# Ragged self-attention on one core: the four-tile sequences get 64-row projections, a rotation of four PSUM banks and attention in groups of 256 query rows

## The chip, the cores and the metric

The kernel runs on one core of a Trainium2 chip. The metric is the device time of one execution in microseconds (us). It is compared with runs of the kernel before on the same chip; before the change the median is 339.91 us (three runs, 339.87 to 341.66).

## What is computed

There are 32 sequences of random length from 64 to 511, each padded to 512 rows of 512 numbers. For each one the kernel computes Q, K and V, softmax attention in 8 heads of 64, and writes the result; rows beyond the length are zero.

```python
for b in range(batch):
    seq_len = lengths[b]
    x_b = x[b, :seq_len].copy()
    qkv = np.matmul(x_b, w_qkv)                       # 512 -> 3 * 512
    q, k, v = np.split(qkv, 3, axis=-1)               # each to [head, seq, 64]
    scores = scale * np.matmul(q, k.transpose(0, 2, 1))
    attn = np.exp(scores - max) ; attn = attn / (sum + 1e-08)
    output[b, :seq_len] = np.matmul(attn, v) ...      # the rest stays zero
```

The lengths of this case, sorted, are 502 447 446 436 | 363 357 351 347 343 333 323 315 310 261 260 257 | 246 230 223 220 216 183 164 152 143 140 134 119 | 101 86 79 75. The bars part them by how many tiles of 128 rows they fill when taken in pairs: four, three, two and one.

## The kernel before

**Order of work.** The kernel sorts the sequences by length on the chip and handles them in pairs, longest first. A pair runs in a class N, the smallest multiple of 32 (or 340) that holds its longer member; T is N in tiles of 128. Here the classes are 512, 448 (T = 4), 384, 352, 352, 340, 320, 288 (T = 3), 256, 224, 224, 192, 160, 160 (T = 2), 128, 96 (T = 1). The code holds one body per class, and each engine branches from body to body by a register that it loads from the table `cls` (`next_class`, called through `read_class`). A body is two **halves**, one per sequence. In a half the core does the attention of the present sequence (buffers with index h) and, between its steps, the projections of the next one (index g = 1 - h).

**Engines.** TensorE does all matmuls. ScalarE does the exponentials (L344, or L376 in the "dense" T = 3 classes of 340 and less), some casts of Q and K (L407) and half of the output stores. VectorE does the other casts (L408), copies V out of PSUM with the row mask (L431, L479, L499), and normalises the attention output (reciprocal L574, products L593 and L595). GpSimd casts the next x to fp16; SyncE issues the loads, transposes x by DMA into `xT`, and issues the other stores.

**PSUM.** There are eight banks: four in two score slots, `psc` (s0 and s1, two banks each), two in `pa` (a0, a1), two in `pav` (v0, v1). Each has a semaphore that says it was read out: `acquire` makes TensorE wait for it (shown as `e_a0` and so on), `evacuate` raises it.

**The order in a half** is a string of tokens, `ORDER[T]`, or `DENSE`. All engines follow it, each in its own queue:

- `S` is one score unit: for head pair i and key tile kt, two 64-row matmuls over N columns that run side by side (two heads), then one exponential over both banks. Units run i = 1, 2, 3 of this sequence and then i = 0 of the next one. They alternate between s0 and s1, so a unit waits for the exponential of the unit two before it. `D` is a whole dense head pair.
- `Qi` and `Ki` project head pair i of Q or K: four 128-row matmuls over N columns. A small letter has the cast done by ScalarE, a capital one by VectorE.
- `Vi` projects V for key tile i: four 128-row matmuls over 512 columns.
- `Ai` is attention times V for head pair i: per tile of 128 query rows and head, one 65-column matmul per key tile (V has a column of ones for the sum). `+Ai` spreads these between the matmuls of the token before it.
- `O` is the first output store on ScalarE's queue.
- `Ei`/`Fi` .. `Ii` (and `Ui`/`Wi` for V) project two groups at once in 64-row matmuls into two banks: `cross_begin` does rows 0 to 63 of the contraction for one bank side by side with rows 64 to 127 for the other, `cross_end` waits for the semaphore `s_cross` and does the other halves. Only T = 3 used them.

For T = 4 the string before (32 matmuls of the projections of Q and K are 128-row, banks a0 and a1 take turns, attention of a head pair fills both banks of `pav`):

```python
4: "S S Q0 +A0 S S K0 V0 S S Q1 +A1 S S K1 V1 S S Q2 +A2 S S K2 V2 S S Q3 +A3 S S V3 K3 O",
3: "k3 S S E0 E2~ S F0 S I2 S A0 A1 S U0 S S W0 E1~ S S G1 A2 Q3 O A3 S S V2",
DENSE = "K2 q2 D E1 E3 I1 H3 D k0 A0 Q0~ A1 D V2 O V1 A2 D A3~ V0"
```

T = 3 takes its banks "in turns": `pick` pops the bank that has been free longest from the list a0, a1, v0, v1, `give` puts it at the end.

For T = 1 the order is written out in `half`: Q and K of the next sequence in a0 and a1 (which swap from half to half), attention, then all of V in the bank that Q had, then the four score units at once.

Before the first body a prologue projects the first sequence; its last token, V3, is read out of a1 by VectorE.

Of the kernel before, what the change touches and what calls it, by code (L numbers as in the profile page):

```python
# [11 lines left out]
ALU = mybir.AluOpType  # L12

P = 128
NH = 8
HD = 64
NPAIR = 4
# [3 lines left out]
STAGE = 256  # L21
FIRST = {4: 20, 3: 20, 2: 20, 1: None}
AGAIN = 2
SECOND = {4: 20, 3: AGAIN, 2: 0, 1: None}
AT_DENSE = 20
# [123 lines left out]
def kernel(  # L149
# [11 lines left out]
    NC = D // P  # L161
# [8 lines left out]
    def sem(name):  # L170
# [92 lines left out]
        for b in banks  # L263
        for g in (("act",) if b[0] == "s" else ("act", "dve"))
    }
# [25 lines left out]
    def group(pr, b, eng, mms, evac):  # L291
        acquire(pr, b)
        close(pr, b, eng, mms, b[0] != "s")
        evacuate(pr, b, eng, evac)
# [172 lines left out]

    def vproj(pr, bank, h, i, T, whole=False):
        b = f"a{bank}"
        mms = []  # L470
        if whole:
            for c in range(NC):
                mms.append(
                    mm(pa[:, bank, :], xT[h][:, c, 0:P], w_r[:, c, 2 * D : 3 * D],
                       c == 0, c == NC - 1)
                )
            group(
                pr, b, "dve", mms,
                lambda e: e.tensor_scalar(  # L479
                    out=v_aug[h][:, 0, :, 0:HD],  # L480
                    in0=pa[:, bank].rearrange("p (h d) -> p h d", d=HD),
                    scalar1=now[0][:, 0, 0:1], scalar2=None, op0=ALU.mult,
                ),
            )
            return
# [11 lines left out]
        group(  # L497
            pr, b, "dve", mms,
            lambda e: e.tensor_tensor(  # L499
                out=v_aug[h][:, 0:T, 2 * i : 2 * i + 2, 0:HD],  # L500
                in0=pa[:, bank, 0 : T * P].rearrange("p (t a d) -> p t a d", a=2, d=HD),
                in1=now[0][:, 0, 0:T].unsqueeze(2).unsqueeze(3).broadcast_to([P, T, 2, HD]),
                op=ALU.mult,
            ),
        )
# [4 lines left out]

    def attnv(pr, h, i, T, late=False, b=None):

# [6 lines left out]
        if b is not None:  # L519
            jobs = [(2 * 74 * qt, i, qt) for qt in range(T)]  # L520
        elif T == 1:
            jobs = [(74 * 2 * j, j, 0) for j in range(NPAIR)]
        elif T == 4:
            jobs = [(256 * qt, i, qt) for qt in range(T)]
        else:
            jobs = [(74 * (4 * qt + 2 * (i % 2)), i, qt) for qt in range(T)]
        mms = []
        for o0, j, qt in jobs:
            for par in range(2):
                o = o0 + par * (HD + 1 if T == 4 else 74)  # L530
# [15 lines left out]
        if b is not None:  # L546
            res = into[:, 0 : 2 * 74 * T].rearrange("p (t a d) -> p t a d", a=2, d=74)
            dst = on[:, i // 2, 0:T, P * (i % 2) : P * (i % 2 + 1)]
            dst = dst.rearrange("p t (a d) -> p t a d", d=HD)
            sh, fin = [T, 2], i % 2 == 1  # L550
        elif T == 4:
# [5 lines left out]
        else:  # L557
# [4 lines left out]
            else:  # L562
                dst = on[:, i // 2, 0:T, :].rearrange("p t (a d) -> p t a d", d=HD)
        rv = rcp[:, i, 0 : sh[0] * sh[1]].rearrange("p (j a) -> p j a", a=sh[1])
        num, den = res[..., 0:HD], res[..., HD]
# [4 lines left out]
        def recip():  # L570
            for j in (0, 1) if T == 1 else (i // 2,) if not each or i % 2 == 0 else ():
                pr.take("dve", s_od[h][j], 16)
            pr.take("dve", full[(name, "dve")])
            pr.add("dve", lambda e: e.reciprocal(out=rv, in_=den).then_inc(s_r, 1))  # L574

        def mult():
            pr.take("dve", s_r)

            if T == 1:
                cuts = [(slice(0, 2), 0)]  # L580
            elif h == 0:
# [37 lines left out]
    def spread_last(pr):  # L619
# [15 lines left out]
    ORDER = {  # L635
# [3 lines left out]
    }  # L639
    DENSE = "K2 q2 D E1 E3 I1 H3 D k0 A0 Q0~ A1 D V2 O V1 A2 D A3~ V0"  # L640

# [4 lines left out]
    def half(pr, h, T, N, W, st, last=False):  # L646
# [11 lines left out]
        if T == 1:  # L658
            start_proj()
            qk(pr, f"a{st['bank']}", g, [(i, 0) for i in range(NPAIR)], W, P)  # L660
            qk(pr, f"a{st['bank'] ^ 1}", g, [(i, 1) for i in range(NPAIR)], W, P, "act")
            pr.take("pe", s_on[h])
            attnv(pr, h, 0, 1)
            vproj(pr, st["bank"], g, 0, 1, True)
            read_class(pr, h)
            acquire(pr, f"a{st['bank'] ^ 1}")
            pr.signals.append(s_xtf[g])
            if last:
                act_store(pr, h, 0, T)
            scores(pr, h, g, 0, 0, 1, W)  # L670
            if not last:
                act_store(pr, h, 0, T)
            st["bank"] ^= 1
            return
# [19 lines left out]
        for tok in toks:  # L694
# [4 lines left out]
            if k in "SD" and turns:  # L699
# [4 lines left out]
                assert units[0][0] in (1, 2) or len(st["seen"]) == len(area)  # L704
            if k == "S":
                i, kt = units.pop(0)
                scores(pr, st["slot"], *((g, i, kt, T, W) if i == 0 else (h, i, kt, T, N)))
                st["slot"] ^= 1
            elif k == "D":
                i = units[0][0]  # L710
                del units[:T]
                scores_dense(pr, *((g, i, W) if i == 0 else (h, i, N)))
            elif k == "A":
                if first:
# [8 lines left out]
                norm[i] = attnv(pr, h, i, T, f"X{i}" in toks, b)  # L723
                if turns:
# [7 lines left out]
            else:  # L732
# [71 lines left out]
    def in_turns(N):  # L804
        return -(-N // P) == 3 and (not is_dense(N) or "E" in DENSE)

# [964 lines left out]
```

## Time and profile before

| what | value |
|---|---|
| median of the runs shown | 339.91 us |
| the profiled execution: its own time / its span | 339.98 us / 338.2 us |
| TensorE clock granted, mean | 0.996 |
| the T = 4 bodies (first score unit to first T = 3 matmul) | 24.57 to 99.33 us |
| the T = 3 bodies, to the first score unit of T = 2 | 99.33 to 240.35 us |
| the T = 1 bodies | from 319.40 us |

1.8 us of the profiled execution lie outside its span. In the rows, times are microseconds from the start of the span. A timeline row reads: start, busy time of the group from its first start to its last end, engine, line, operation, output<-inputs, shapes, count, and in brackets the idle time ahead with what ended it. Matmuls overlap: the next one starts when the columns of the one before have been streamed in, some 0.16 us before that one's row ends. So the pace of TensorE is read from start to start. `64*128` says that a matmul uses 64 rows of the array.

### The profile page before, as it was taken

The page shows a single profiled execution, that of the slowest core. Times are in us where ns is not written, and L with a number is a line of the kernel's source. Part 1 is how long each engine was busy: PE and PEld are TensorE (multiplying, and loading weights), DVE is VectorE, ACT ScalarE, POOL GpSimd, SP SyncE. Part 2 cuts the span into 40 slices and gives each one's busy share as a digit, 9 for nine tenths or more (in the row PEclk, how much of TensorE's full clock was granted, in tenths as well). Part 3 has the DMA queues.
Part 4 walks back from the last instruction along what each step waited for, and adds up shares of the span by engine and source line. Part 5 has one row for each costly group of instructions (what it writes and reads, how often), then busy time and mean ns, then how long its engine had stood idle before and what let it go on. Part 6 is the DMA issues. An engine that isn't in the chain of part 4 may idle for free. (4 is left out here: it accounts for less than half of the span.)

```text
span 338.2 us, 12070 instructions
## 1 busy us (share of the span) xinstructions
PE 326.1 (96%) x4286; PEld 206.7 (61%) x4287; DVE 211.4 (63%) x560; ACT 239.9 (71%) x337; POOL 63.5 (19%) x102
## 2 busy tenths in 40 slices
PE   7999999999999999999999999999999999999992
PEld 2665454555545656566666676667677777776761
DVE  3676567665665566567557556745766666766772
ACT  4568787777779877977877887777776666556541
POOL 3634020202010220220221022012111221121241
PEclk9999999999999999999999999999999999999998
DMA  6977799866855986886787888898898666988731
GB/s 207 349 161 230 205 392 222 287 165 212 162 188 150 286 292 148 268 302 205 221 292 267 191 251 298 154 255 194 213 171 188 203 162 153 185 193 148 180 111 68
DMA packets 82272, 72.10 MB, mean 213 GB/s; under 512 B 40652, under 2 KB 63180, under 8 KB 82196
## 3 DMA queue, kind: packets, MB, share of 16 engines
q1 hardware_dynamic: 70340, 59.61, 67.3%
q10 hardware_dynamic: 11856, 11.54, 9.9%
q8 instruction: 40, 0.66, 0.8%
q14 instruction: 36, 0.29, 0.3%
HBM read 25.32 MB, written 36.70 MB: 183 GB/s over the span
## 5 line engine op out<-in xcount | busy, mean ns | idle before, releaser
L344 ACT ACTIVATE ep<-psc 128x704 f16<-128x704 f32 (+7 forms) x193 | 156.8, 858 | 58.0 <-PE psc L302 41.0
L302 PE MATMUL pa<-xT,w_r 128*128 128x224 f16 (+21 forms) x984 | 134.2, 276 | 2.3 <-PEq L57 0.9
L302 PEld LDWEIGHTS pa<-xT,w_r 128*128 128x128 f16 (+1 forms) x984 | 75.0, 97 | 35.6 <-issue 14.8
L408 DVE CAST qkT<-pa 128x448 f16<-128x448 f32 (+9 forms) x85 | 48.8, 575 | 47.1 <-PE pa L302 46.5
L302 PE MATMUL pa<-w_r,xT 128*128 128x512 f16 (+3 forms) x348 | 69.9, 346 | 0.0
L302 PE MATMUL psc<-qkT 64*128 64x352 f16 (+17 forms) x702 | 66.9, 287 | 1.2 <-ACT ep L376 0.5
L302 PE MATMUL pav<-v_aug,ep 128*128 128x65 f16 x1414 | 62.1, 194 | 0.0
L302 PEld LDWEIGHTS pav<-v_aug,ep 128*128 128x128 f16 x1414 | 55.4, 98 | 9.3 <-issue 1.1
L1610 POOL CAST v_aug<-masks 128x24 f16 (+4 forms) x33 | 9.1, 276 | 244.5 <-POOLq L1239 244.5
L595 DVE SCALAR_TENSOR_TENSOR onat<-pav,masks,rcp 128x128 f32<-128x128 f32 (+2 forms) x137 | 48.2, 391 | 5.2 <-DVE rcp L574 2.1
L376 ACT ACTIVATE ep<-psc 128x960 f16<-128x960 f32 (+3 forms) x48 | 43.4, 962 | 10.7 <-PE psc L302 7.5
L431 DVE TENSOR_TENSOR v_aug<-pa,masks 128x512 f16<-128x512 f32 (+1 forms) x58 | 39.0, 677 | 17.9 <-PE pa L302 16.9
L1605 POOL CAST x<-x_nat 128x1536 f16<-128x1536 f32 (+3 forms) x33 | 42.1, 1274 | 9.8 <-POOLq L1239 9.3
L302 PEld LDWEIGHTS psc<-qkT 64*128 64x128 f16 x702 | 25.6, 94 | 29.7 <-issue 20.8
L302 PE MATMUL pav<-xT,w_r 64*128 64x352 f16 (+10 forms) x328 | 43.6, 300 | 0.0
L302 PEld LDWEIGHTS pa<-w_r,xT 128*128 128x128 f16 (+1 forms) x348 | 26.0, 97 | 22.3 <-issue 4.4
L407 ACT CAST qkT<-pa 128x352 f16<-128x352 f32 (+7 forms) x58 | 26.5, 462 | 16.0 <-ACTq L57 8.5
L302 PEld LDWEIGHTS pav<-xT,w_r 64*128 64x128 f16 (+1 forms) x328 | 23.6, 95 | 9.4 <-issue 1.1
L574 DVE RECIPROCAL rcp<-pav 128x8 f32<-128x8 f32 (+1 forms) x71 | 14.1, 198 | 22.6 <-PE pav L302 17.2
L302 PE MATMUL pav<-w_r,xT 128*128 128x512 f16 (+2 forms) x84 | 20.7, 374 | 0.0
L302 PEld LDWEIGHTS pa<-v_aug,ep 128*128 128x128 f16 x378 | 13.6, 98 | 4.2 <-issue 1.8
L593 DVE TENSOR_TENSOR onat<-pav,rcp 128x256 f32<-128x256 f32 (+1 forms) x32 | 14.6, 458 | 1.1
(77 smaller groups left out, 132.8 us busy)
## 6 DMA issues: line engine op xcount, KB each, us to landing
out_dram<-zt SPq DMA_DIRECT2D x16, 768.0 KB, 5.8
x_nat<-in_x_dram SPq DMA_DIRECT2D x12, 512.0 KB
x_nat<-in_x_dram SPq DMA_DIRECT2D x5, 1024.0 KB
out_dram<-onat ACTq DMA_DIRECT2D x12, 384.0 KB, 5.0
out_dram<-onat SPq DMA_DIRECT2D x12, 384.0 KB, 4.3
x_nat<-in_x_dram SPq DMA_DIRECT2D x17, 256.0 KB, 6.2
out_dram<-onat ACTq DMA_DIRECT2D x16, 256.0 KB, 3.2
x_nat<-in_x_dram SPq DMA_DIRECT2D x4, 768.0 KB
```

The source lines that it names most:

```text
L302: return lambda e: e.matmul(o, lhsT, rhs, start=start, stop=stop)
L344: lambda e: e.activation(out=dst, in_=src, func=AF.Exp, scale=scale),
L376: lambda e, par=par, b=b: e.activation(out=ep[:, i, par, 0:3, 0:N], in_=psc_f[:, par, 0 : 3 * N].rearrange("p (t n) -> p t n", n=N), func= ...
L407: return lambda e: e.copy(out=dst, in_=src)
L408: return lambda e: e.tensor_copy(out=dst, in_=src)
L431: return lambda e: e.tensor_tensor(out=v_aug[h][:, t, lo // HD : lo // HD + n, 0:HD], in0=area[b][:, 0:w].rearrange("p (a d) -> p a d", d=HD),
L574: pr.add("dve", lambda e: e.reciprocal(out=rv, in_=den).then_inc(s_r, 1))
L593: ins = e.tensor_tensor(op=ALU.mult, **ops)
L595: ins = e.scalar_tensor_tensor(scalar=now[0][:, 1, t : t + 1], op0=ALU.mult, op1=ALU.mult, **ops)
L1605: e.tensor_copy(out=x16[h][:, 0:T, :], in_=x_nat[h][:, 0:T, :]).then_inc(s_xc[h], 1)
L1610: e.tensor_copy(out=v_aug[h][:, 0:T, :, HD], in_=src[:, 0, 0:T].unsqueeze(2).broadcast_to([P, T, NH]),).then_inc(s_on[h], 1)
```

## The change

T = 4 gets a new order and takes its banks in turns like T = 3. Q and K of a head pair are one `E` and one `G` (Q is then cast by VectorE, K by ScalarE). Attention of a head pair comes in two pieces, `A` for query tiles 0 and 1 and `Z` for tiles 2 and 3, each in one bank. Each engine's normalisation is cut accordingly: per head pair two reciprocals and, in the first half, three products in place of two.

```diff
-        4: "S S Q0 +A0 S S K0 V0 S S Q1 +A1 S S K1 V1 S S Q2 +A2 S S K2 V2 S S Q3 +A3 S S V3 K3 O",
+        4: "S E1 S G1 S E2 S G2 S E0 S E3 S G0 G3 S S A0 Z0 V1 +A1 S S Z1 V3 +A2 S O S V0 +Z2 S A3 Z3 S S V2",
...
-    DENSE = "K2 q2 D E1 E3 I1 H3 D k0 A0 Q0~ A1 D V2 O V1 A2 D A3~ V0"
+    DENSE = "K2 q2 D E1 E3 I1 H3 D k0 c A0 Q0~ A1 D V2 O V1 A2 D A3~ V0"
...
     def in_turns(N):
-        return -(-N // P) == 3 and (not is_dense(N) or "E" in DENSE)
+        return -(-N // P) >= 3
...
-            elif k == "A":
+            elif k in "AZ":
...
+                cut = 2 if T == 4 else T
+                qts = range(cut) if k == "A" else range(cut, T)
+                norm[i] = attnv(pr, h, i, T, f"X{i}" in toks, b, qts)
...
+            if k == "c":
+                read_class(pr, h)
...
-                    if was < (3 if T == 2 else 2) <= dones:
+                    if "c" not in toks and was < (3 if T == 2 else 2) <= dones:
                         read_class(pr, h)
...
-FIRST = {4: 20, 3: 20, 2: 20, 1: None}
+FIRST = {4: 4, 3: 20, 2: 20, 1: None}
-SECOND = {4: 20, 3: AGAIN, 2: 0, 1: None}
+SECOND = {4: 4, 3: AGAIN, 2: 0, 1: None}
```

`FIRST` and `SECOND` place the start of a half's code of TensorE in a block of 256 bytes. The dense classes get the token `c`: the class register is loaded there, and no longer right after q2. T = 1 loses the swap of a0 and a1, and V goes through a score slot, with VectorE reading it out:

```diff
-            qk(pr, f"a{st['bank']}", g, [(i, 0) for i in range(NPAIR)], W, P)
-            qk(pr, f"a{st['bank'] ^ 1}", g, [(i, 1) for i in range(NPAIR)], W, P, "act")
+            qk(pr, "a0", g, [(i, 0) for i in range(NPAIR)], W, P)
+            qk(pr, "a1", g, [(i, 1) for i in range(NPAIR)], W, P, "act")
             pr.take("pe", s_on[h])
             attnv(pr, h, 0, 1)
-            vproj(pr, st["bank"], g, 0, 1, True)
+            vwhole(pr, g)
             read_class(pr, h)
-            acquire(pr, f"a{st['bank'] ^ 1}")
+            for b in ("a0", "a1"):
+                acquire(pr, b)
...
+    def vwhole(pr, h):
+        into = psc[:, h, 0, :]
+        mms = [
+            mm(into, xT[h][:, c, 0:P], w_r[:, c, 2 * D : 3 * D], c == 0, c == NC - 1)
+            for c in range(NC)
+        ]
+        group(
+            pr, f"s{h}", "dve", mms,
...
```

**TensorE, the first tokens of a T = 4 body.** A row is a line of the code, the operation, output<-inputs and columns; `waits` names semaphores. Before:

```order
L302 MATMUL psc<-qkT 128x512 [waits e_s0]
L302 MATMUL psc<-qkT 128x512
L302 MATMUL psc<-qkT 128x512 [waits e_s1]
L302 MATMUL psc<-qkT 128x512
L302 MATMUL pa<-xT,w_r 128x512 [waits s_xt1,e_a0,s_on0,e_v0,e_v1]
L302 MATMUL pav<-v_aug,ep 128x65 x8
L302 MATMUL pa<-xT,w_r 128x512
L302 MATMUL pav<-v_aug,ep 128x65 x8
```

And now:

```order
L302 MATMUL psc<-qkT 128x512 [waits e_s0]
L302 MATMUL psc<-qkT 128x512
L302 MATMUL pa<-xT,w_r 128x512 [waits s_xt1,e_a1,e_a0]
L302 MATMUL pa<-xT,w_r 128x512 x7
L1139 REGISTER_ALU
L1140 BRANCH_PREFETCH_HINT
L302 MATMUL psc<-qkT 128x512 [waits e_s1]
L302 MATMUL psc<-qkT 128x512
L302 MATMUL pa<-xT,w_r 128x512 [waits s_cross]
L302 MATMUL pa<-xT,w_r 128x512 x7
L302 MATMUL psc<-qkT 128x512 [waits e_s0]
```

Two score units stood together and a 128-row group followed; now one unit is followed by eight 64-row matmuls into two banks, which wait for both banks at once, and the second eight wait for the first through `s_cross`. Attention (128x65) begins only after nine units.

**ScalarE, the same place.** Before, 16 exponentials with the class load between; now the first tokens put two casts of K between them:

```order
L344 ACTIVATE ep<-psc 128x2x512 [waits f_s0_act]
L344 ACTIVATE ep<-psc 128x2x512 [waits f_s1_act]
L407 CAST qkT<-pa 128x512 [waits f_a1_act]
L1083 ISA
L1086 TENSOR_LOAD cls
L344 ACTIVATE ep<-psc 128x2x512 [waits f_s0_act]
L344 ACTIVATE ep<-psc 128x2x512 [waits f_s1_act]
L407 CAST qkT<-pav 128x512 [waits f_v1_act]
```

Each half has four such casts on ScalarE's queue, in order between the exponentials; they were VectorE's.

**ScalarE at the start of a dense T = 3 body** (class 340). Before:

```order
L407 CAST qkT<-pa 128x340 [waits f_a1_act]
L1071 ISA
L1074 TENSOR_LOAD cls
L376 ACTIVATE ep<-psc 128x3x340 [waits f_s0_act]
L376 ACTIVATE ep<-psc 128x3x340 [waits f_s1_act]
```

And now:

```order
L407 CAST qkT<-pa 128x340 [waits f_a1_act]
L376 ACTIVATE ep<-psc 128x3x340 [waits f_s0_act]
L376 ACTIVATE ep<-psc 128x3x340 [waits f_s1_act]
L407 CAST qkT<-pav 128x340 [waits f_v0_act]
L407 CAST qkT<-pav 128x340 [waits f_v1_act]
L407 CAST qkT<-pa 128x340 [waits f_a0_act]
L376 ACTIVATE ep<-psc 128x3x340 [waits f_s0_act]
L376 ACTIVATE ep<-psc 128x3x340 [waits f_s1_act]
L407 CAST qkT<-pav 128x340 [waits f_v0_act]
L1083 ISA
L1086 TENSOR_LOAD cls
```

The load of the class register (`TENSOR_LOAD cls`) stood between the first cast and the first exponentials; it now stands behind the second pair of them and one more cast.

More of the change, by code (lines that the diff above doesn't have):

```diff
@@ L263 @@
         for b in banks
-        for g in (("act",) if b[0] == "s" else ("act", "dve"))
+        for g in ("act", "dve")
     }
@@ L292, in group @@
         acquire(pr, b)
-        close(pr, b, eng, mms, b[0] != "s")
+        close(pr, b, eng, mms, b[0] != "s" or eng == "dve")
         evacuate(pr, b, eng, evac)
@@ L466, in cross_end, with vproj @@
             evacuate(pr, b, eng, out_(b, eng))
-    def vproj(pr, bank, h, i, T, whole=False):
+    def vwhole(pr, h):
[6 more added lines that the diff above has]
+            pr, f"s{h}", "dve", mms,
+            lambda e: e.tensor_scalar(
+                out=v_aug[h][:, 0, :, 0:HD],
+                in0=into.rearrange("p (h d) -> p h d", d=HD),
+                scalar1=now[0][:, 0, 0:1], scalar2=None, op0=ALU.mult,
+            ),
+        )
+    def vproj(pr, bank, h, i, T):
         b = f"a{bank}"
         mms = []
[L471 to L485, printed above, removed]
         for t in range(T):
@@ L509, in vtile, with attnv @@
         group(pr, b, "dve", v_mms(b, h, i, T, of), v_out(b, h, i, T, of))
-    def attnv(pr, h, i, T, late=False, b=None):
+    def attnv(pr, h, i, T, late=False, b=None, qts=None):
         for s_ in ("s0", "s1"):
@@ L519, in attnv @@
         if b is not None:
-            jobs = [(2 * 74 * qt, i, qt) for qt in range(T)]
+            jobs = [(2 * 74 * k, i, qt) for k, qt in enumerate(qts)]
         elif T == 1:
@@ L529, in attnv @@
             for par in range(2):
-                o = o0 + par * (HD + 1 if T == 4 else 74)
+                o = o0 + par * (HD + 1 if T == 4 and b is None else 74)
                 into = pav if b is None else area[b]
@@ L546, in attnv @@
         if b is not None:
-            res = into[:, 0 : 2 * 74 * T].rearrange("p (t a d) -> p t a d", a=2, d=74)
-            dst = on[:, i // 2, 0:T, P * (i % 2) : P * (i % 2 + 1)]
+            n = len(qts)
+            res = into[:, 0 : 2 * 74 * n].rearrange("p (t a d) -> p t a d", a=2, d=74)
+            dst = on[:, i // 2, qts[0] : qts[0] + n, P * (i % 2) : P * (i % 2 + 1)]
             dst = dst.rearrange("p t (a d) -> p t a d", d=HD)
-            sh, fin = [T, 2], i % 2 == 1
+            sh, fin = [n, 2], i % 2 == 1 and T - 1 in qts
         elif T == 4:
@@ L563, in attnv @@
                 dst = on[:, i // 2, 0:T, :].rearrange("p t (a d) -> p t a d", d=HD)
-        rv = rcp[:, i, 0 : sh[0] * sh[1]].rearrange("p (j a) -> p j a", a=sh[1])
+        r0 = 2 * qts[0] if b is not None else 0
+        rv = rcp[:, i, r0 : r0 + sh[0] * sh[1]].rearrange("p (j a) -> p j a", a=sh[1])
         num, den = res[..., 0:HD], res[..., HD]
@@ L570, in recip @@
         def recip():
-            for j in (0, 1) if T == 1 else (i // 2,) if not each or i % 2 == 0 else ():
+            opens = i % 2 == 0 and (b is None or 0 in qts)
+            for j in (0, 1) if T == 1 else (i // 2,) if not each or opens else ():
                 pr.take("dve", s_od[h][j], 16)
@@ L580, in mult @@
                 cuts = [(slice(0, 2), 0)]
+            elif b is not None:
+                whole = [] if h else [k for k, t in enumerate(qts) if t < T - 1]
+                cuts = [(slice(0, len(whole)), None)] if whole else []
+                cuts += [(slice(k, k + 1), t) for k, t in enumerate(qts) if k not in whole]
             elif h == 0:
@@ L672, in half @@
                 act_store(pr, h, 0, T)
-            st["bank"] ^= 1
             return
@@ L704, in half @@
                 assert units[0][0] in (1, 2) or len(st["seen"]) == len(area)
-            if k == "S":
+            if k == "c":
+                read_class(pr, h)
+            elif k == "S":
                 i, kt = units.pop(0)
```

1 line of the change is left out of this document (removed).

## The prediction

> **What bounds the kernel now.** I read the page's shares first, then the stretches, then the timeline of one half of each kind.
>
> ```profile
> PE 326.1 (96%) x4286; PEld 206.7 (61%) x4287; DVE 211.4 (63%) x560; ACT 239.9 (71%) x337; POOL 63.5 (19%) x102
> 40.00:60.00 20.00, 20.00 (x229) 10.36 (x228) 12.65 (x31) 16.46 (x18) 2.21 (x2) 1.00 1.15 317
> 100.00:120.00 20.00, 20.00 (x281) 11.90 (x282) 10.63 (x33) 17.71 (x27) 3.40 (x4) 1.00 0.83 214
> ```
>
> TensorE is busy all the time in the T = 4 stretch (40 to 60) and in the T = 3 stretch (100 to 120), at full clock, so only what shortens its own queue counts. But busy is not peak pace. The timeline of class 512 gives the pace:
>
> ```profile
> 35.78 1.02 ACT L344 ACTIVATE ep<-psc 128x1024 f16<-128x1024 f32 x1
> 36.90 0.61 PE L302 MATMUL psc<-qkT 64*128 64x512 f16 x4
> 37.33 1.94 ACT L344 ACTIVATE ep<-psc 128x1024 f16<-128x1024 f32 x2 [0.53 <-PE psc L302]
> 37.43 1.04 PE L302 MATMUL pa<-xT,w_r 128*128 128x512 f16 x4
> 38.31 1.03 PE L302 MATMUL pa<-w_r,xT 128*128 128x512 f16 x4
> 39.27 0.61 PE L302 MATMUL psc<-qkT 64*128 64x512 f16 x4
> 39.70 1.94 ACT L344 ACTIVATE ep<-psc 128x1024 f16<-128x1024 f32 x2 [0.43 <-PE psc L302]
> ```
>
> A group of four 128-row matmuls takes 38.31 - 37.43 = 0.88 us, 0.22 each. Two score units should take 2 x 0.22 = 0.44, yet the next group starts after 0.53 (36.90 to 37.43); and V at 38.31 is followed by scores after 0.96, not 0.88. So about 0.1 is lost each time between the 64-row scores and 128-row work. ScalarE waits for TensorE ahead of each pair of exponentials (0.53, 0.43): it has room. Class 384, which already has the new form, shows the loss alone:
>
> ```profile
> 103.35 0.33 PE L302 MATMUL psc<-qkT 64*128 64x384 f16 x2
> 103.61 0.73 PE L302 MATMUL pa<-v_aug,ep 128*128 128x65 f16 x18
> 104.17 0.71 PE L302 MATMUL pav<-v_aug,ep 128*128 128x65 f16 x18
> 104.82 0.34 PE L302 MATMUL psc<-qkT 64*128 64x384 f16 x2
> 104.99 0.38 PE L302 MATMUL pa<-w_r,xT 64*128 64x512 f16 x1
> 105.86 0.54 PE L302 MATMUL psc<-qkT 64*128 64x384 f16 x4
> ```
>
> From 64 to 128 rows: the unit at 103.35 streams 0.16 (as 104.82 to 104.99 does) but attention starts 0.26 later: 0.10 lost. From 128 to 64: 18 attention matmuls take 0.56, then the same 18 take 0.65: 0.09 lost. Between the unit at 104.82 and the 64-row group at 104.99 nothing is lost. And that group, eight 64-row matmuls over 512 columns in pairs, takes 105.86 - 104.99 = 0.87: as long as four 128-row ones.
>
> **Part by part.** *Projections as E and G.* Streaming costs the same (0.87 per group either way), so 64 rows gain nothing by themselves. What goes is the changes between row modes. Before, a half has 8 pairs of units among 128-row work: 16 changes. The new order has five 64-row stretches (the first nine units with all E and G; S S; S S, with the store between; S; S S): 10 changes. Saved: 6 x 0.10 x 4 halves = **2.4 us**.
>
> The Trainium skill states it as a rule, in TensorEngine Tiling (Array Packing), Key Properties: a change of tiling mode drains the array. TensorE: Matmul & The Clock Gate, Single matmul latency, has about 175 ns for a drain; by that price the 24 changes would be an estimated 4.2 us. The rows here say 0.10, not 0.175, and the sum goes by them.
>
> *The wait between E and G* is new at this distance. In class 384 the same wait exists:
>
> ```profile
> 117.36 1.03 PE L302 MATMUL pa<-w_r,xT 64*128 64x512 f16 x8
> 118.47 0.66 PEld L302 LDWEIGHTS pa<-w_r,xT 64*128 64x128 f16 x8
> 321.48 0.59 ACT L407 CAST qkT<-pa 128x512 f16<-128x512 f32 x1 [1.04 <-ACTq L57]
> 43.57 0.41 ACTq L1247 DMA_DIRECT2D out_dram<-onat  x1
> ```
>
> The first eight end at 118.39, the weights of the second eight load at 118.47: 0.08 later. A row ends 0.16 after its columns are in (1.03 against 0.87), so G's weights load 0.24 after E's columns, while only one unit of 0.22 (0.19 at 448) stands between. So TensorE idles at least 0.02 and at most that plus one weight load (0.66 for eight in pairs that overlap streaming; a single one about 0.1): 0.02 to 0.13. I take 0.05, near the lower end since loads overlap streaming everywhere in these rows. G1 and G2 in four halves: **-0.4** (bounds -0.2 and -1.0). G0 and G3 have a whole E between and cost nothing.
>
> TensorE: Matmul & The Clock Gate of the Trainium skill, The cost: per-tile semaphore tail, speaks against E here: two increments on two tiles leave an estimated tail of 87 ns. The 0.08 agrees; by it the least stall would be 0.03, and the eight would cost 0.25.
>
> *Four casts a half on ScalarE.* Exponentials follow each other at 1.94 - 1.02 = 0.92; a cast of 512 columns is 0.59, and with the same overlap of 0.1 it takes 0.50. In the first stretch ScalarE has 9 x 0.92 + 4 x 0.50 = 10.3, TensorE 9 x 0.22 + 8 x 0.87 = 8.9. So ScalarE falls 1.4 behind. A unit waits only for the exponential two before it, so up to 2 x 0.92 = 1.84 is free. Behind unit 9, A0, Z0, V1 and A1 give it 48 x 0.031 + 0.87 = 2.3 without a score. Later the store's issue (0.41, the last row) stands between exponentials 12 and 13; if I follow both queues from there, exponential 14 ends 0.14 after unit 16 could start. I charge 0.15 a half: **-0.6** (bounds 0, and the slow rival below). What is queued behind such a late unit is all of TensorE.
>
> *The start of the first half and the two ends.*
>
> ```profile
> 24.57 0.60 PE L302 MATMUL psc<-qkT 64*128 64x512 f16 x4
> 24.79 0.69 DVE L499 TENSOR_TENSOR v_aug<-pa,masks 128x512 f16<-128x512 f32 x1
> 25.29 0.38 PE L302 MATMUL pa<-xT,w_r 128*128 128x512 f16 x1
> 44.97 4.69 SPq L1324 DMA_TRANSPOSE xT<-x  x1
> 63.75 0.35 PE L302 MATMUL pa<-xT,w_r 128*128 128x448 f16 x1 [0.18 <-PEq L57]
> 99.33 0.82 PE L302 MATMUL pa<-xT,w_r 128*128 128x384 f16 x4 [0.30 <-DVE v_aug L431]
> ```
>
> E1 needs a0 and a1; a1 is read out by VectorE until 25.48. So E1 starts at about 25.53 with one unit done, where Q0 started at 25.29 with two done: 0.24 + 0.22 = **-0.46**. At 63.75 four semaphore steps in a row on TensorE's sequencer cost 0.18; the new order meets fewer at one place: **+0.18**. At 99.33 the first T = 3 group waits 0.30 for a0, which held V3 at the end of T = 4; the new order ends with V2 in v1, and a0 is long free: **+0.3**. T = 4 and its end together: 2.4 - 0.4 - 0.6 - 0.46 + 0.18 + 0.3 = **1.4**.
>
> *At nothing:* the finer normalisation (4 reciprocals and some products more a half, against four casts of 0.69 less; VectorE is busy 12.65 of 20, and the other three banks cover it; without that cover each wait for a bank is a reciprocal and two products, about 0.9). xT is asked for one unit earlier, 0.2 us, by DMAs that start at 44.97 for a half that starts at 63. The start of a half's code moves by 16 bytes: no row prices it, the four entries show at most 0.18.
>
> *Dense T = 3.* The class load leaves the place ahead of the first exponentials.
>
> ```profile
> 219.66 0.54 PE L302 MATMUL psc<-qkT 64*128 64x288 f16 x8
> 219.77 0.40 ACT L407 CAST qkT<-pa 128x288 f16<-128x288 f32 x1 [0.73 <-PE pa L302]
> 220.83 1.67 ACT L376 ACTIVATE ep<-psc 128x864 f16<-128x864 f32 x2 [0.67 <-PE psc L302]
> 222.65 0.55 PE L302 MATMUL psc<-qkT 64*128 64x288 f16 x8 [0.48 <-ACT ep L376]
> 173.62 0.61 PE L302 MATMUL psc<-qkT 64*128 64x340 f16 x8
> 174.45 1.93 ACT L376 ACTIVATE ep<-psc 128x1020 f16<-128x1020 f32 x2 [0.28 <-PE psc L302]
> ```
>
> In class 288 the scores end at 220.20 and the cast at 220.17, yet the exponential starts at 220.83: 0.63 in which ScalarE has nothing but that load, and TensorE's next scores then wait 0.48. Class 340: scores end at 174.23, the exponential starts 0.22 later. I count **+0.5** (bounds 0, if the load's time in its new place is caught by something else, and 0.6).
>
> *T = 1.* V no longer holds the bank that K needs next.
>
> ```profile
> 322.74 1.66 PE L302 MATMUL pa<-xT,w_r 128*128 128x96 f16 x32
> 324.23 0.42 PE L302 MATMUL pav<-v_aug,ep 128*128 128x65 f16 x8
> 325.79 1.80 PE L302 MATMUL pa<-xT,w_r 128*128 128x96 f16 x32
> 327.43 0.42 PE L302 MATMUL pav<-v_aug,ep 128*128 128x65 f16 x8
> 329.13 0.81 ACT L344 ACTIVATE ep<-psc 128x768 f16<-128x768 f32 x1 [0.91 <-ACTq L57]
> 329.77 0.64 PE L302 MATMUL pa<-xT,w_r 128*128 128x64 f16 x16 [0.21 <-DVE v_aug L479]
> 330.24 0.42 PE L302 MATMUL pav<-v_aug,ep 128*128 128x65 f16 x8
> ```
>
> The third half takes 1.64 from projection to attention, the second 1.49: 0.15. In the last, attention at 330.24 could start when the exponential ends, 329.94: 0.3 less. Each lies on the chain to the last store. I count **+0.3** of 0.45.
>
> The sum: 1.4 + 0.5 + 0.3 = 2.2. The profiled execution took 339.98, 0.07 over the median of 339.91, so the median should become **337.8 us** (337.7 by the sum, rounded up, since what is not counted mostly costs).
>
> **The rivals.** *Nothing comes of T = 4* (0.20): the waits for s_cross cost 0.13 and ScalarE is late 0.3 a half: 2.4 - 1.0 - 1.2 - 0.28 + 0.3 = 0.2, and only half of the 0.8 outside T = 4 arrives: 339.3. For it: both sizes are bounds, not rows. Against: T = 3 loses nothing at its E and G.
>
> *ScalarE becomes the bound of T = 4* (0.13), the slow side. If exponentials and casts in turn follow each other only at their full 1.02 and 0.59, the first stretch costs it 9 x 1.02 + 4 x 0.59 = 11.5 against 8.9: 2.6 late, 0.8 more than the 1.84 that the two slots allow, and about 0.3 more at the half's end: 1.1 a half, 4.4 in place of 0.6. That gives 337.8 + 3.8 = 341.6; it decides from a pace of about 2.5 for two exponentials and a cast. For it: 17.71 of 20 us at T = 3. Against: there TensorE keeps its pace.
>
> *The waits cost nothing* (0.12): cross and ScalarE terms at zero, the rest at its upper bounds: 2.4 - 0.46 + 0.18 + 0.3 + 0.6 + 0.45 = 3.5, so 336.4. That the change doesn't do what it says is ruled out by the orders shown.
>
> **How the numbers follow.** The forecast has 0.55, its own range 336.8 to 338.8. About 0.5% (1.7 us) is what a measurement can tell from no change: the border is 338.2. Faster by more: 0.43 of the forecast's 0.55, the free case 0.12, 0.01 of the others: 0.56. Within: 0.12 of the forecast, 0.19 of the first rival, 0.03 of the slow one: 0.34, the rest, 0.10, is slower. The range of 8 in 10 is 336.3 to 340.2: it takes in the first rival and the free case and leaves out the slow one.
>
> **What would show it.** Right: in the T = 4 stretch no idle time between a score unit and an E; G1 and G2 starting within 0.3 of E's last column; the 74.8 from 24.57 to 99.33 down to about 73.4; the T = 3 start without its 0.30; in class 288 an exponential within 0.1 of the end of its scores. Wrong: score units of TensorE waiting for ScalarE's ep in every half, more than 0.3 at a G, or idle time on TensorE's sequencer at the entries of the halves.

## The result, and the profile after

On one chip the changed kernel took 341.31 us (median of 22 runs, 339.51 to 344.98), the kernel before 341.0 us (22 runs, 339.4 to 343.29). The ratio is 0.9999 with a 95% interval of 0.998 to 1.0019, that is -0.7 to +0.65 us. The ratio and its interval leave out executions that are more than 1.5% above the fastest of their kernel, here the one of 344.98 us. A second comparison gave 1.0007 (0.9988 to 1.0027). So nothing came of the forecast 2.2 us, and 341.31 lies above the range. Of the 3.5 us between the forecast 337.8 and 341.31, 1.1 is the kernel before itself: its median is 341.0 in these runs and was 339.91 when the forecast was made.

The page and two windows of the changed kernel, to be held against the rows of the prediction (start and end, length, then busy time and count of PE, PEld, DVE, ACT and POOL, granted clock, DMA share, GB/s):

```profile
PE 325.1 (95%) x4414; PEld 208.8 (61%) x4415; DVE 206.0 (60%) x576; ACT 246.4 (72%) x353; POOL 62.9 (18%) x102
40.00:60.00 20.00, 18.43 (x240) 9.85 (x236) 10.30 (x32) 17.25 (x20) 2.13 (x2) 1.00 1.07 317
100.00:120.00 20.00, 20.00 (x274) 11.80 (x274) 11.53 (x37) 17.70 (x28) 3.40 (x4) 1.00 0.73 200
```

In the T = 4 stretch TensorE was busy 20.00 of 20 us before; now it idles for 1.57. The span of this profile is 343.2 us; 3.3 of it come from a late input of T = 1, which befalls the kernel before too (below), so the stages are compared over several profiles. The table gives, from the starts of TensorE's rows, T = 4 (first score unit to first T = 3 projection), T = 3 (from there to the first scores over 256 columns), T = 1 (from the 96-column scores to the 64-column scores), and the rest to the end of the span.

```
profiles of                          T = 4                  T = 3                   T = 1 (96 to 64)   rest
the kernel before (3)                74.76 74.70 74.87      139.06 138.79 138.82    6.22 6.22 6.22     6.48 6.29 6.29
the changed kernel (3)               75.83 75.73 75.67      138.24 138.40 138.39    6.00 5.94 5.78     7.78 7.66 7.54
```

T = 4 was to become 1.4 shorter and is 1.0 longer. T = 3 is 0.5 shorter, T = 1 0.3 shorter, both as forecast. The list of what TensorE waits for from 24 to 99.2 us (total, times, longest) shows what is new in T = 4. The kernel before had one entry:

```profile
PE pa L302 <- PEq L57: 0.2, 1, 0.2
```

The changed kernel has four:

```profile
PE psc L302 <- ACT ep L344: 1.4, 2, 0.9
PE pa L302 <- DVE v_aug L500: 0.7, 1, 0.7
PE psc L302 <- PEq L57: 0.5, 1, 0.5
PE psc L302 <- issue: 0.2, 1, 0.2
```

The timeline of TensorE and of ScalarE at the place in the first half:

```profile
39.63 0.60 PE L302 MATMUL psc<-qkT 64*128 64x512 f16 x4
...
42.44 0.65 PE L302 MATMUL pav<-v_aug,ep 128*128 128x65 f16 x16
43.96 0.39 PE L302 MATMUL psc<-qkT 64*128 64x512 f16 x2 [0.86 <-ACT ep L344]
44.87 0.39 PE L302 MATMUL psc<-qkT 64*128 64x512 f16 x2 [0.53 <-ACT ep L344]
...
64.27 0.38 PE L302 MATMUL psc<-qkT 64*128 64x480 f16 x2 [0.46 <-PEq L57]
```

```profile
40.06 1.02 ACT L344 ACTIVATE ep<-psc 128x1024 f16<-128x1024 f32 x1 [0.54 <-PE psc L302]
42.08 0.41 ACTq L1259 DMA_DIRECT2D out_dram<-onat  x1
42.88 3.77 ACT L344 ACTIVATE ep<-psc 128x1024 f16<-128x1024 f32 x4 [1.79 <-ACTq L57]
```

Between exponential 12 (ends 41.08) and 13 (42.88) ScalarE has nothing but the token `O`, and waits 1.79 on its own queue. The scores of units 12 and 13 were done at 40.23 (the first row). The store's issue is 0.41 of that. Ahead of it the trace records a register load from the table `idx` that runs from 40.15 to 41.74, 1.59 us: `act_store` begins with `act_index`, which reads the number of the sequence whose rows go out. The load starts while exponential 12 (1.02) runs, so what of the token fits under that exponential costs nothing, and the rest holds up exponential 13. Units 15 and 16 then wait for the score slots of 13 and 14, 0.86 and 0.53. In the second half the same load takes 0.93, and unit 16 waits 0.46; the view puts this down to TensorE's sequencer (PEq), but exponential 14, which frees the slot, ends at 64.12. In the other two halves the load takes 0.28, and no unit waits. The last entry, `issue`, is a unit at 48.62 that stands behind TensorE's own load of the class register (47.65 to 48.57).

### The profile page after: what moved, and what is told of

Same layout as the page of the kernel before. It is cut to its first block, busy times and chain, and to the rows that moved or that the text cites. A ratio compares the mean times of both kernels' runs of the same rounds, so it can differ in the third digit from the quotient of the medians.

```text
span 343.2 us, 12396 instructions
## 1 busy us (share of the span) xinstructions
PE 325.1 (95%) x4414; PEld 208.8 (61%) x4415; DVE 206.0 (60%) x576; ACT 246.4 (72%) x353; POOL 62.9 (18%) x102
## 5 line engine op out<-in xcount | busy, mean ns | idle before, releaser
L302 PE MATMUL pa<-xT,w_r 128*128 128x224 f16 (+22 forms) x984 | 111.0, 276 | 4.7 <-PEq L57 2.7
L408 DVE CAST qkT<-pa 128x320 f16<-128x320 f32 (+9 forms) x61 | 33.4, 549 | 42.5 <-PE pa L302 39.9
L302 PE MATMUL pav<-xT,w_r 64*128 64x352 f16 (+14 forms) x456 | 58.8, 316 | 0.0
L302 PE MATMUL pa<-w_r,xT 128*128 128x512 f16 (+3 forms) x284 | 54.9, 338 | 0.0
L302 PE MATMUL pav<-v_aug,ep 128*128 128x65 f16 x1094 | 48.1, 194 | 0.2 <-PEq L57 0.2
L302 PEld LDWEIGHTS pav<-v_aug,ep 128*128 128x128 f16 x1094 | 42.8, 98 | 7.1 <-issue 1.4
L407 ACT CAST qkT<-pa 128x352 f16<-128x352 f32 (+9 forms) x66 | 31.1, 475 | 16.8 <-PE pa L302 8.2
L302 PE MATMUL pav<-w_r,xT 128*128 128x512 f16 (+2 forms) x132 | 36.0, 377 | 0.0
L302 PE MATMUL pa<-v_aug,ep 128*128 128x65 f16 x698 | 29.6, 194 | 0.0
L578 DVE RECIPROCAL rcp<-pav 128x6 f32<-128x6 f32 (+2 forms) x67 | 13.0, 193 | 21.8 <-PE pav L302 16.1
```

The source lines that it names most:

```text
L302: return lambda e: e.matmul(o, lhsT, rhs, start=start, stop=stop)
L407: return lambda e: e.copy(out=dst, in_=src)
L408: return lambda e: e.tensor_copy(out=dst, in_=src)
```

## The experiments

**The changed kernel again.**

> The changed kernel unchanged, for a second profile. Theory (T = 4 gives back on ScalarE what it saves: the index load of 0.3 to 1.6 us and the store's issue of 0.41 stand between exponentials 12 and 13): again 1 to 2 us of waits for ScalarE's ep in the first two halves of T = 4, where the index load is longest, none in the last two; about 1.3 us net of these saved between the first score unit of T = 4 and the T = 3 start. Rival (the T = 1 tail eats the gain): the tail from the end of T = 2 to the last store is again 2 us or more longer than in the kernel before, with the second T = 1 projection waiting for its transposed input. Rival (chance of one execution): neither shows again. Time: 340 to 341.5 by all of them.

340.99 us (12 runs) against 340.37. Score units again wait behind late exponentials: 0.77 and 0.53 in the first half, 0.23 and 0.48 in the second, nothing in the others. T = 4 took 75.73; without these 2.0 us it would be 73.7, 1.1 under the kernel before, where 1.3 was expected. The T = 1 wait did not come back. The load and the wait go together in all profiles that have the load at this place:

```
                            first half: load, waits of units 15 and 16    second half: load, waits
the changed kernel          1.59   0.86 + 0.53                            0.93   0.46
the same, second profile    1.49   0.77 + 0.53                            1.26   0.23 + 0.48
the same, third profile     1.56   0.95 + 0.52                            0.96   0.48
casts on VectorE (below)    0.88   0.41                                   0.44   none
```

**The load moved.** First load and store together to the end of the half, as in the old order; then the load alone, into the idle time behind exponential 9.

```diff
-... +A1 S S Z1 V3 +A2 S O S V0 +Z2 S A3 Z3 S S V2
+... +A1 S S Z1 V3 +A2 S S V0 +Z2 S A3 Z3 S S V2 O
```

> Index load and output store of a T = 4 half moved from behind exponential 12 to the half's end. Theory (they block ScalarE's queue): the waits for ep at score units 15 and 16 go, 1.4 + 0.5 us, so 1.5 to 2 us below the changed kernel, about 339.3 against 341.3. Rival (T = 4 has nothing to give, TensorE's own queue sets its end): within 0.5 us of the changed kernel. Rival (ScalarE is the bound over the whole half): the wait moves to the next half's first units, and the gain is under 0.5 us.

```diff
-... S S A0 Z0 V1 +A1 ...
+... S S A0 y Z0 V1 +A1 ...
+            elif k == "y":
+                pr.add("act", act_index)
...
-                act_store(pr, h, 0, T)
+                act_store(pr, h, 0, T, T != 4)
```

> Only the index load moved, to behind exponential 9, where ScalarE is idle while TensorE does A0 to A1; the store's issue stays between exponentials 12 and 13. Theory (the load is what costs, the 0.41 of the store fits within the slack of two score slots): within 0.4 us of the kernel with both moved. Rival (the store's issue costs as much): halfway, 0.8 to 1 us below the changed kernel. Rival (neither matters): within 0.5 us of the changed kernel.

With both at the end: 339.64 us, 0.997 of the kernel before (0.9952 to 0.9988), T = 4 74.57. With the load alone moved: 338.85 us, 0.995 (0.9931 to 0.9969), T = 4 73.37. I had expected the two within 0.4 us of each other; they are 0.8 apart. ScalarE's timeline around exponential 12, and then all that TensorE waits for from 24 to 99.2 us, of the second of these kernels:

```profile
40.64 1.02 ACT L344 ACTIVATE ep<-psc 128x1024 f16<-128x1024 f32 x1 [0.54 <-PE psc L302]
40.87 0.41 ACTq L1261 DMA_DIRECT2D out_dram<-onat  x1
41.67 1.99 ACT L344 ACTIVATE ep<-psc 128x1024 f16<-128x1024 f32 x2
```

```profile
PE pa L302 <- DVE v_aug L500: 0.7, 1, 0.7
```

The store's issue now runs under exponential 12, and the next exponential starts as soon as this one ends. Every wait for `ep` is gone, so the store in its new place costs nothing and the load is the whole loss: 75.74 - 73.37 = 2.4 us in T = 4. Half by half, against the mean of the three profiles of the changed kernel, it is 1.50, 0.86, -0.08 and 0.09: all of it lies where the load is long. With both at the half's end a load is again followed by work that is due: there the class load at the next half's start took 1.06 us, and a unit waited 0.29 for `ep`. On TensorE two score units waited 0.24 and 0.29 behind its own class load. These are 0.8 of the 1.2 by which it is longer than the other.

**The parts outside T = 4 alone**, the token `c` and the T = 1 code put into the kernel before.

> The kernel before with the two parts outside T = 4 alone: the class load of dense T = 3 one place later, and the T = 1 banks. By the sum of the prediction 0.5 + 0.3 = 0.8 us faster than the kernel before. If the T = 1 tail lost as in the one profile of the changed kernel: 1.5 to 3 us slower. If neither matters: within 0.5 us.

339.59 against 340.37 us; 0.9982 (0.996 to 1.0004). The medians differ by the forecast 0.8, but the interval reaches to no change. In the profile T = 3 took 138.46, T = 1 5.92, and T = 4 74.71 as before.

**The price of a change between row modes.** On the kernel with the early load, Q and K again as whole 128-row groups in the same places.

```diff
-4: "S E1 S G1 S E2 S G2 S E0 S E3 S G0 G3 S S A0 y Z0 ...
+4: "S Q1 S k1 S Q2 S k2 S Q0 S Q3 S k0 k3 S S A0 y Z0 ...
```

> The kernel with the early index load, with each Q or K of T = 4 again as one whole group of four 128-row matmuls on one of the four banks that go round (Q cast on VectorE, K on ScalarE as there). Per half 14 more changes between 64 and 128 rows. Theory (a change costs 0.09 to 0.10): 56 x 0.095 = 5.3 longer, less 0.2 for the waits between the two 64-row halves of a group and 0.4 because the first half's first group needs one bank instead of two: the T = 4 stretch from 73.4 to about 78, the time from 338.9 to about 343. Rival (the changes cost nothing, the earlier gain came from the order of the rest): within 0.5 us of the kernel with the early index load, the T = 4 stretch 73 to 74.

346.62 us, 1.0162 of the kernel before (1.0125 to 1.0199), more than the 343 expected. The profiled execution, 344.69, is among the two shortest of the six. Its T = 4 took 79.57. TensorE has one idle time in it:

```profile
47.25 0.39 PE L302 MATMUL psc<-qkT 64*128 64x512 f16 x2 [1.95 <-issue]
```

That is the entry of the second half; the trace has the time as one branch of TensorE's sequencer, from 43.83 to 47.19, which takes 0.35 to 0.45 in the other profiles. Without the 1.95, T = 4 would be 77.62, that is 4.25 over 73.37. The whole groups also save two things. In the kernel with the early load the first E starts 1.06 after the first unit (25.40 and 26.46), 0.85 more than a unit needs; and the waits between E and G (0.04 to 0.07 each, below) are gone, 0.44 in all. So the 56 extra changes cost 4.25 + 0.85 + 0.44 = 5.54: 0.099 each, the 0.10 of the prediction. That they cost nothing is ruled out.

**The first group's banks.** On the kernel with the early load, the four banks go round from another start, v0 first or v1 first.

```diff
-"banks": list(area), ...
+"banks": list(area)[2:] + list(area)[:2] if T == 4 else list(area), ...
```

> The kernel with the early index load, with the four banks of T = 4 taken in the order v0, v1, a0, a1 in place of a0, a1, v0, v1. Theory (the first group waits for a1, which VectorE still reads for the prologue's last V): the wait of 0.3 to 0.7 us ahead of the first E goes, T = 4 from 73.4 to 72.7 to 73.0, and the T = 3 start stays without a wait, since Z3 leaves a0 more than 1 us earlier. Time 0.5 us below 338.9, unless the T = 1 stage, which waits for its transposed input, takes it back: then equal. Rival (the wait only moves, to G1 or to the scores of the next unit): T = 4 unchanged.

```diff
-"banks": list(area), ...
+"banks": list(area)[3:] + list(area)[:3] if T == 4 else list(area), ...
```

> The kernel with the early index load, with the four banks of T = 4 taken in the order v1, a0, a1, v0: the first group finds v1 and a0, which the prologue has left before, and Z3 at the end of T = 4 stands in a1, so a0 is free for T = 3. Theory: neither the wait of 0.67 ahead of the first E nor the 0.31 at the T = 3 start; the T = 4 stretch (to the first T = 3 projection) 72.6 to 72.9. Rival (one of the two waits only moves): 73.2 or more. Time 338.4 to 339 where the kernel before has 340.4 to 341.3.

v0 first: 339.86 against 341.3 us, 0.9939 (0.9914 to 0.9964), T = 4 73.21. The first E no longer waits, but the T = 3 start then waits 0.31 for a0, which Z3 left late: most of the wait moved. My expectation had denied that. v1 first: 337.86 us against 340.98, 0.9904 (0.9872 to 0.9937), T = 4 72.85. TensorE's start and the T = 3 start have no wait there:

```profile
25.67 0.39 PE L302 MATMUL psc<-qkT 64*128 64x512 f16 x2
26.09 0.37 PE L302 MATMUL pav<-xT,w_r 64*128 64x512 f16 x1
...
98.52 0.81 PE L302 MATMUL pa<-xT,w_r 128*128 128x384 f16 x4
```

**Both casts on VectorE**, with the load where the change has it.

```diff
-S E1 S G1 S E2 S G2 S E0 S E3 S G0 G3 S S ...
+S E1 S F1 S E2 S F2 S E0 S E3 S F0 F3 S S ...
```

> The changed kernel (index load still behind exponential 12) with both casts of each pair on VectorE. ScalarE has 4 x 0.5 = 2.0 us a half less. Theory (ScalarE has caught up long before unit 12, so the casts are not what makes units 15 and 16 late; the load is): the waits of 1 to 1.9 us for ep in the first two halves stay, T = 4 75.2 to 75.9, time within 0.5 us of the changed kernel. Rival (four casts a half make ScalarE the bound): the waits go, T = 4 about 73.5, time 1.5 to 2 us lower.

342.94 against 341.3 us, 1.0069 (1.0042 to 1.0096); T = 4 76.94. Both expectations missed. TensorE's waits in T = 4:

```profile
PE pav L302 <- DVE qkT L408: 1.6, 7, 0.3
PE pa L302 <- DVE v_aug L500: 0.7, 1, 0.7
PE psc L302 <- ACT ep L344: 0.4, 1, 0.4
```

VectorE now gives the banks back late. The wait for `ep` is short here, but so was the load in this execution (0.88 and 0.44), so this run does not part casts and load. The one with the load moved does: there all four casts stay on ScalarE, and no wait for `ep` is left.

**The load twice** in the changed kernel.

```diff
+        if j == 0 and T == 4:
+            pr.add("act", lambda e: batch_of(e, regs_act["rank"], regs_act["tmp"], 0))
         if j == 0:
             pr.add("act", act_index)
```

> The changed kernel with the index load of T = 4 done twice at its place behind exponential 12. Theory (that load blocks ScalarE's queue and with it score units 15 and 16): each half gets 0.35 (the shortest load seen, 0.28, and its register steps) to 1.6 us more on ScalarE at that place, and TensorE loses nearly all of it where it already waited, in the first two halves: T = 4 stretch 75.8 + 1 to 3 = 77 to 79. Rival (the load is not on the path): 75.5 to 76.

The trace has 49 register loads on ScalarE, as many as without the edit: the unused first load is not in the compiled program. So this tells nothing of doubling; it is the third profile of the changed kernel above (T = 4 75.67).

**T = 1.** Its part alone in the kernel before, and two more profiles of the kernel before.

> The kernel before with the T = 1 part alone. By the prediction 0.3 us faster than the kernel before. Theory formed from the profiles (T = 1 is paced by its transposed input, which arrives 0.4 us or less ahead of its use in the kernel before): no gain, within 0.3 us, and in some executions a wait of 1.5 to 2 us for it. Rival (V in the score banks delays the scores): 0.5 us or more slower.

> The kernel before, for a second profile of its T = 1 stage. Theory (the transposed input of the second T = 1 half comes late by chance of the DMA engines, in this kernel too): in some executions 128-column scores to 96-column scores take 11 to 12.6 in place of 9.3, with a wait of 1.5 to 2 us ahead of the second projection. Rival (the T = 1 part of the change makes it late): 9.2 to 9.4 in every profile of this kernel.

> As the run before it, a third profile of the kernel before: 9.3 or 11 to 12.6 in the T = 1 stage by the theory, always 9.2 to 9.4 by the rival.

T = 1 alone: 340.82 against 341.3 us, 0.9979 (0.9955 to 1.0003), so within what can be told from nothing. Two more executions of the kernel before took 339.59 and 342.71. In the second of them, the second T = 1 projection waits for its transposed input:

```profile
325.81 0.88 PE L302 MATMUL pa<-xT,w_r 128*128 128x96 f16 x17 [1.81 <-PEq L57]
```

From the 128-column to the 96-column scores it took 11.26 us; in the other two profiles of that kernel 9.26. The changed kernel's profiles have 12.58, 9.36 and 9.39. So a late input there is not the change's doing, though in its first profile it cost 3.3 and in the kernel before 2.0. The trace marks the landing of a transfer in 16 parts; one part of that transpose landed at 324.80, the others by 322.87; a DMA packet that the trace calls instruction, of 16 KiB, was moved from 322.44 to 323.50, but that this is the cause is not shown.

**The best version with the old and with the new T = 1 code**, on one chip.

```diff
-            qk(pr, "a0", g, [(i, 0) for i in range(NPAIR)], W, P)
-            qk(pr, "a1", g, [(i, 1) for i in range(NPAIR)], W, P, "act")
+            qk(pr, f"a{st['bank']}", g, [(i, 0) for i in range(NPAIR)], W, P)
+            qk(pr, f"a{st['bank'] ^ 1}", g, [(i, 1) for i in range(NPAIR)], W, P, "act")
...
-            vwhole(pr, g)
+            vproj(pr, st["bank"], g, 0, 1, True)
```

> The kernel with the early index load and the banks v1, a0, a1, v0, with the T = 1 code of the kernel before. Theory (the T = 1 part gains 0.28 up to the last scores and loses more behind them): 96-column scores to 64-column scores 6.2, last scores to the end 6.3 to 6.5 as in the kernel before, and the time 0.3 to 1 us below the same kernel with the new T = 1 part. Rival (the end scatters whatever the T = 1 code, as it does among the kernels that have it): last scores to the end up to 7.5 here too, the time 0.3 above.

> The kernel with the early index load and the banks v1, a0, a1, v0 again, beside the one before it on the same chip: T = 4 stretch 72.7 to 73.0, time 337.5 to 339 and 0.8 to 1.2 % below the kernel before.

Old T = 1 code: 338.7 us, 0.9897 of the kernel before (0.9849 to 0.9945). New: 339.06 us, 0.9941 (0.9906 to 0.9977). The intervals overlap. Here the old code too needs 7.26 us from the last scores to the end (new: 7.93), so the longer rest does not come from the T = 1 part alone. The T = 4 stretch was 73.01 and 73.44; the second, like its time, is a little above what I expected. In both a unit of the second half waits behind TensorE's own class load (1.01 and 1.12 us), 0.27 and 0.39.

## Why the prediction was wrong

**The step that failed** is the late ScalarE: "Later the store's issue (0.41, the last row) stands between exponentials 12 and 13 ... I charge 0.15 a half: -0.6". I counted one instruction of the token `O` and left out the one ahead of it, a register load. In the old order `O` stood behind a half's last exponential, so its load, 0.68 to 0.99 us in the first half there too, held nothing up. The new order puts an exponential that is due behind it. The load keeps ScalarE's queue for 1.5 to 1.6 us in the first half and 0.9 to 1.3 in the second. Moving it alone takes 2.4 us off T = 4, where the term had 0.6; the store's 0.41, which was charged, costs nothing, because without the load it is issued under exponential 12. So a forecast gain of 1.4 in T = 4 became a loss of 1.0. What I named as a sign of being wrong came: score units waiting for `ep`, though in two halves and not in every one. The Trainium skill has a figure of about 0.6 us as the floor of such a load (DMA: Bandwidth & Descriptors, Latency and other measured facts). The trace does not bear it out: 37 of the changed kernel's 49 loads on ScalarE took less than 0.32, and one 1.59.

**The other steps** held, with one agreement by luck.

- *Mode changes, 2.4:* 0.099 each by the run with whole groups, where 0.10 was used.
- *The sum for T = 4, 1.4:* with the load out of the way T = 4 is 74.78 - 73.37 = 1.4 shorter, just that sum. This is luck: the sum holds 0.6 for a late ScalarE, which that kernel does not pay, so the other terms should have given 2.0. Half by half they gave 0.04, 0.50, 0.68 and 0.80; measured against the first profile before are -0.17, 0.27, 0.59 and 0.70. Of the missing 0.6, 0.1 is the first E, which starts 1.06 after the first unit where 0.96 was forecast; the rest is not traced.
- *The wait between E and G, 0.05:* the timeline of the changed kernel at the start of T = 4:

```profile
24.82 0.39 PE L302 MATMUL psc<-qkT 64*128 64x512 f16 x2
25.88 1.04 PE L302 MATMUL pa<-xT,w_r 64*128 64x512 f16 x8 [0.67 <-DVE v_aug L500]
26.74 0.40 PE L302 MATMUL psc<-qkT 64*128 64x512 f16 x2
26.99 1.04 PE L302 MATMUL pa<-xT,w_r 64*128 64x512 f16 x8
```

  E's columns end 0.87 after 25.88, G starts 0.24 later, within the 0.3 named. From the unit between them (26.74) to G it is 0.25, where the next unit, which no wait follows, needs 0.21 (27.87 to 28.08, the second E): 0.04 is lost. In class 448 it is 0.26 (66.50 to 66.76) against 0.19: 0.07. The eight cost 0.4 together, as forecast.
- *The first half, -0.46:* the wait for a1 is the 0.67 above. Banks that are free at that time made T = 4 shorter by 73.37 - 72.85 = 0.5.
- *The two ends, +0.18 and +0.3:* the 448 entry and the T = 3 start have no wait in the changed kernel.
- *Dense T = 3, +0.5:* in class 288 ScalarE and TensorE now run

```profile
220.85 0.40 ACT L407 CAST qkT<-pa 128x288 f16<-128x288 f32 x1 [0.74 <-PE pa L302]
221.33 1.67 ACT L376 ACTIVATE ep<-psc 128x864 f16<-128x864 f32 x2
```

```profile
220.75 0.54 PE L302 MATMUL psc<-qkT 64*128 64x288 f16 x8
223.14 0.55 PE L302 MATMUL psc<-qkT 64*128 64x288 f16 x8
```

  The exponential starts 0.08 after the cast's end, where it had been 0.66, and the next scores wait for nothing. The whole T = 3 stretch is 138.95 in the mean of the four profiles without the token `c` and 138.39 in the twelve with it: 0.56.
- *T = 1, +0.3:* right up to the last scores (6.22 to 5.9 in the mean; the old code on the turned banks had 6.02), and not seen in the time. Behind them the rest of the span is 6.3 to 6.5 in the kernel before and 6.6 to 7.9 in all others, with either T = 1 code. There the end waits for the last store. Its issue ends 0.2 later after the last scores than in the kernel before, and it lands 3.5 to 3.8 us after that, against 2.5 to 2.7. In each profile 15 of its 16 parts land within 2.3; the last one lands 1.3 to 1.6 after the end of a DMA packet that the trace calls instruction, of 16 KiB (339.05 and 340.55 in the first profile of the changed kernel, 334.00 and 335.50 in that of the kernel before). In the one profile without such a packet, that with both casts on VectorE, all land within 1.9. Why the packet comes later with the new code is open.
- *At nothing:* the finer normalisation made no wait. The place of a half's code does not always cost nothing: 1.95 at an entry in the run with whole groups, against my bound of 0.18. The Trainium skill says that a taken branch to code that is not yet there stalls until it is fetched (Runtime: NRT & Kernel Launch, Instruction fetch mechanics). The trace agrees as far as it goes: the 1.95 lies within a branch, and while it lasts an instruction packet of 16 KiB is moved, from 44.85 to 45.81. That the branch waits for this packet is not shown.

**The rivals.** "ScalarE becomes the bound" gave 341.6, close to what came, by the wrong mechanism: its exponentials and casts keep pace through the first nine units, and with the load moved and the casts left in place no unit waits for `ep`. "Nothing comes of T = 4" had a wait of 0.13 at each G, which is 0.04 to 0.07, and ScalarE late in every half, which it is in two. "The waits cost nothing" is out: the G's cost 0.4. The true rival was one that I did not list, a register load on ScalarE's queue.

**The balance.** Over three profiles each, T = 4 is 0.96 longer, T = 3 0.54 and T = 1 0.31 shorter, and the rest 1.31 longer, 1.4 in all, while the runs say -0.7 to +0.65. Without the rest the three stages add up to +0.1. The rest is the last store, which the prediction had not looked at; it takes 6.6 to 7.9 us in profiles of other kernels with the new T = 1 code, so three profiles may not give its mean. The gap is not closed.

## What to carry to other kernels

When a step moves in an engine's queue, list every instruction it issues, register loads and address work too, and ask what stands behind each in the new place; a load that was free at the end of a stage can cost more than all that the new order saves. Read its longest duration in the trace, not its median, and put it where the engine is idle anyway. The version with the load moved and the banks turned is 0.6 to 1.0% faster than the kernel before (ratios 0.9904, 0.9872 to 0.9937, and 0.9941, 0.9906 to 0.9977), where the changed kernel has 0.9999.

## What the runs showed of the hardware

- A register load of one number from an on-chip table took 0.27 to 1.59 us on ScalarE, and what stood behind it in that queue waited for it. How full the DMA engines are does not explain it alone. Windows of the second profile of the changed kernel (the last two columns are DMA share and GB/s):

```profile
39.00:41.00 2.00, 2.00 (x28) 1.04 (x24) 1.21 (x3) 1.02 (x1) 0.00 (x0) 1.00 1.02 337
60.00:61.00 1.00, 1.00 (x18) 0.65 (x17) 0.92 (x4) 0.90 (x1) 0.00 (x0) 1.00 0.84 213
78.00:79.00 1.00, 1.00 (x15) 0.46 (x14) 0.77 (x2) 0.45 (x1) 0.00 (x0) 1.00 0.97 367
```

  The loads that began in these windows took 1.49 (at 39.6), 1.26 (at 60.0) and 0.28 (at 78.6).
- A change between 64-row and 128-row matmuls on TensorE cost 0.10 us (56 more of them, 5.54 us).
- One DMA transpose in T = 1 lands late in some executions, before and after the change: TensorE then waits 1.7 to 2.1 us for it, and the way from the 128-column to the 96-column scores takes 1.7 to 3.3 us longer.
- The last of a store's 16 parts can land up to 1.9 us after the others; it did so behind an instruction packet of 16 KiB (above).
